# Sliding-window copy: the large DMA packets of all three rings doubled in size, and the direct ring's mix of copies made uniform

## The chip, the cores and the metric

The kernel runs on one core of a Trainium2 chip. The metric is the device time of the core in microseconds. Runs of one kernel mostly agree within 0.3%, and all runs used here are of the fast state or, where a kernel ran once, of unknown state (said there).

## The reference

Every batch of 4096 rows of 256 floats is cut into 127 overlapping windows of 64 rows, 32 rows apart. Nothing is computed; it is all copying.

```python
def setup_inputs():
    batch, length, dim = (32, 4096, 256)
    window_size = 64
    stride = 32
    return {'x': np.random.randn(batch, length, dim).astype(np.float32), 'window_size': window_size, 'stride': stride}

def reference(x, window_size, stride):
    batch, length, dim = x.shape
    n_windows = (length - window_size) // stride + 1
    result = np.zeros((batch, n_windows, window_size, dim), dtype=np.float32)
    for i in range(n_windows):
        start = i * stride
        result[:, i] = x[:, start:start + window_size].copy()
    return result
```

A block of 32 rows is 32 KB and lies twice in the output (but for the ends). A window is 64 KB, contiguous in the input and in the output. The output has 266 MB.

## The kernel before

All work is done by DMA. Three queues ("rings") feed the same 16 DMA engines, each engine having its own share of each ring:

- The **direct ring** (issued by SP) copies windows of 20 batches from HBM to HBM. A byte of output is one byte moved, one read of HBM and one write.
- The **staged ring** (issued by ACT) takes 12 batches through SBUF: one load of 4 MB and two stores of 4 MB each (blocks as first and as second halves of windows). Six tiles are loaded, then stored, then six more. A byte of output is 1.5 bytes moved, but only half a read and one write of HBM.
- The **late ring** (issued by GpSimd, a software ring) copies the windows of direct batches that staged stores overrun, 15 windows a batch, when the direct ring is nearly done.

```python
DIRECT, IN, OUT = 32768, 16384, 16384          # largest packet of each kind, bytes
...
    def windows(self, q, b, w0, n, half=None, piece=DIRECT):
        blk = self.blk
        row = [1, 2 * blk if half is None else blk]
        h = half or 0
        return q.dma_start(
            out=self.oap((b * self.nw + w0) * 2 + h, [[2 * blk, n], row]),
            in_=self.xap(b * self.nb + w0 + h, [[blk, n], row]),
            max_dma_last_dim=piece,
        )
...
    per, loads, stores = 6, 6 * 17, 34
    todo = 7 * len(direct)
    turns = share = 0
    with tc.tile_critical():
        st.run(ring_s)

        for b in direct:
            w = 0 if b - 1 not in staged else 8 if b + 1 in staged and b + 1 < B - 1 else 15
            for j in range(7):
                todo -= 1
                sem = near if todo == 2 else done
                share += 120 if turns % (loads + per * stores) < loads else 88
                if share >= 120:
                    share -= 120
                    turns += 4
                    count(c.windows(ring_d, b, w, 16, 0), done)
                    count(c.windows(ring_d, b, w, 16, 1), sem)
                else:
                    turns += 3
                    count(c.windows(ring_d, b, w, 16), sem)
                w += 16
                # ... (two small copies near the end)
        ring_r.wait_ge(near, 16)
        pieces = (32768,)
        # ... (the late ring: 15, 8 or 7 windows of each direct batch)
```

A copy of 16 windows gives each engine one window: two packets of 32 KB and one packet of 4 bytes that posts the semaphore, three turns of the ring. As two half copies it gives two packets and two semaphore packets, four turns. The code mixes the two forms, 120 of 120 halves while the staged ring loads and 88 of 120 while it stores, and so sets how many bytes the direct ring moves per turn, beside a staged ring that takes turns with it.

## Time and profile before

| | before |
|---|---|
| time, median of the first 3 runs | 753.6 us (753.49 to 754.83) |
| bytes moved by the engines | 317.56 MB |
| packets | 19,698 |
| HBM read and written | 216.86 + 267.19 MB |

From the profile's page of the kernel before: the engines' busy tenths and GB/s moved in 40 slices, then packets, MB and share of engine time by ring (q1 direct, q10 staged, q0 late), then HBM traffic:

```profile
DMA  9999999999999999999999999999999999999995
GB/s 378 429 434 434 432 423 437 422 428 430 433 439 432 426 428 437 432 423 431 424 426 433 437 433 434 427 429 429 429 433 442 425 427 431 443 426 429 420 429 223
DMA packets 19698, 317.56 MB, mean 424 GB/s; under 512 B 5214, under 2 KB 5214, under 8 KB 5422
...
q10 hardware_dynamic: 9792, 151.00, 47.2%
q1 hardware_dynamic: 8688, 147.01, 45.8%
q0 software_dynamic: 1216, 19.53, 6.1%
...
HBM read 216.86 MB, written 267.19 MB: 646 GB/s over the span
```

The engines are full until the last slice.

By stretch (window in us, its length, POOL busy, granted clock, DMA share, GB/s moved). The first two rows and the last lie in stretches in which the staged ring loads, the third in one in which it stores:

```profile
25.00:75.00 50.00, 0.00 (x0) 1.00 1.00 431
75.00:125.00 50.00, 0.00 (x0) 1.00 1.00 427
150.00:375.00 225.00, 0.00 (x0) 1.00 1.01 431
400.00:500.00 100.00, 0.00 (x0) 1.00 1.00 431
```

The rate is even, about 430 GB/s in loads and in stores alike. And the end of the run:

```profile
720.00:740.00 20.00, 0.00 (x0) 1.00 0.98 420
740.00:745.00 5.00, 0.00 (x0) 1.00 0.09 32
745.00:750.00 5.00, 0.00 (x0) 1.00 0.06 22
```

The engines stop nearly together at 740 us; one or two are some us late, and the last two windows follow.

The packet records give more:

- **The line.** Medians of a packet's duration: 4 KB 159 ns, 16 KB 611, 32 KB 1213, that is 8.5 ns plus bytes at 27.2 B/ns. A packet above its line is called slow here, and "excess" is the sum of what packets take above 611, 1213 and (later) 2418 ns, divided by 16 engines.

### The profile page before, as it was taken

To read this page: it belongs to the slowest core of one execution; us is meant where nothing else is said; L and a number is where in the kernel's file an instruction comes from. 1 tells how busy PE (TensorE), PEld (TensorE's weight loads), DVE (VectorE), ACT (ScalarE), POOL (GpSimd) and SP (SyncE) were. 2 spreads that over 40 slices of the span, in tenths; PEclk is the share of its full clock that TensorE was granted. 3 is DMA by queue.
4 is the path that set the end of the run, shared out by engine and by line. 5 is a ranking of instruction groups with operands and counts; after the bars stand their busy time and mean duration, and the time that the engine had idled before them with its cause. 6 is when DMAs were issued, how large, how long until landed. Compare 5 with 4: busy or idle time off the path is not lost.

```text
span 749.0 us, 374 instructions
## 1 busy us (share of the span) xinstructions
POOL 13.6 (2%) x27
## 2 busy tenths in 40 slices
POOL 0000000000000000000000000000000000230100
DMA  9999999999999999999999999999999999999995
GB/s 378 429 434 434 432 423 437 422 428 430 433 439 432 426 428 437 432 423 431 424 426 433 437 433 434 427 429 429 429 433 442 425 427 431 443 426 429 420 429 223
DMA packets 19698, 317.56 MB, mean 424 GB/s; under 512 B 5214, under 2 KB 5214, under 8 KB 5422
## 3 DMA queue, kind: packets, MB, share of 16 engines
q10 hardware_dynamic: 9792, 151.00, 47.2%
q1 hardware_dynamic: 8688, 147.01, 45.8%
q0 software_dynamic: 1216, 19.53, 6.1%
q14 instruction: 2, 0.02, 0.0%
HBM read 216.86 MB, written 267.19 MB: 646 GB/s over the span
## 4 chain that ended last, share of the span: by engine, by line
another core or an unknown queue 93%; POOL 2%; issue 0%; POOLq 0%; SPq 0%
POOL out_dram L34 2%; POOL out_dram L44 0%; POOLq L214 0%; SPq L141 0%; POOLq L94 0%
## 5 line engine op out<-in xcount | busy, mean ns | idle before, releaser
L34 POOL DMA_DIRECT2D out_dram<-in_x_dram x22 | 12.8, 585 | 695.3 <-DMA out_dram<-in_x_dram 649.7
L44 POOL DMA_DIRECT2D out_dram<-in_x_dram x1 | 0.6, 571 | 0.0
L200 POOL MEMSET const-float32-0.0<- 128x1 f32 x1 | 0.1, 98 | 0.2 <-issue 0.2
L200 POOL MEMSET const-bfloat16-1.0<- 128x1 bf16 x1 | 0.1, 102 | 0.0
L200 POOL MEMSET const-float32-1.0<- 128x1 f32 x1 | 0.1, 98 | 0.0
L200 POOL MEMSET const-uint8-127<- 128x1 uint8 x1 | 0.1, 98 | 0.0
## 6 DMA issues: line engine op xcount, KB each, us to landing
out_dram<-in_x_dram SPq DMA_DIRECT2D x232, 512.0 KB, 87.6
out_dram<-xb ACTq DMA_DIRECT2D x24, 4096.0 KB, 128.5
xb<-in_x_dram ACTq DMA_DIRECT2D x12, 4096.0 KB, 119.7
out_dram<-in_x_dram SPq DMA_DIRECT2D x24, 1024.0 KB, 89.6
out_dram<-in_x_dram POOLq DMA_DIRECT2D x17, 960.0 KB, 37.1
out_dram<-in_x_dram POOLq DMA_DIRECT2D x2, 512.0 KB, 43.1
out_dram<-in_x_dram POOLq DMA_DIRECT2D x2, 448.0 KB, 46.0
out_dram<-in_x_dram POOLq DMA_DIRECT2D x1, 576.0 KB, 35.4
```

The source lines that it names most:

```text
L34: return q.dma_start(out=self.oap((b * self.nw + w0) * 2 + h, [[2 * blk, n], row]), in_=self.xap(b * self.nb + w0 + h, [[blk, n], row]), m ...
L44: return q.dma_start(out=self.oap((b * self.nw + w0) * 2, [[part, 16], [2 * self.blk, n], row]), in_=self.xap(b * self.nb + w0, [[part, 16 ...
L200: nc = _bacc.Bacc("TRN2", target_bir_lowering=False, num_devices=1)
```

## The change

Twice the packet size everywhere: 64 KB direct, 32 KB staged, 64 KB late. The intent is fewer packets and half the turns on both rings, so that the balance of the rings stays. As 16 windows are then two turns (one packet, one semaphore), the two forms of copy are replaced by copies of 16 windows with, every eleventh or so, one of 32; the mix no longer depends on whether the staged ring loads or stores.

```diff
--- before.py
+++ after.py
@@ -6,7 +6,7 @@
 from concourse._compat import with_exitstack
 
 
-DIRECT, IN, OUT = 32768, 16384, 16384
+DIRECT, IN, OUT = 65536, 32768, 32768
 
 
 class Copier:
@@ -135,34 +135,31 @@
         dma.then_inc(sem, 16)
         total[sem] += 16
 
-    per, loads, stores = 6, 6 * 17, 34
     todo = 7 * len(direct)
-    turns = share = 0
+    share, singles = 0, False
     with tc.tile_critical():
         st.run(ring_s)
 
         for b in direct:
             w = 0 if b - 1 not in staged else 8 if b + 1 in staged and b + 1 < B - 1 else 15
-            for j in range(7):
-                todo -= 1
-                sem = near if todo == 2 else done
-                share += 120 if turns % (loads + per * stores) < loads else 88
-                if share >= 120:
+            wend = w + 112
+            while w < wend:
+                share += 11
+                n = 16
+                if share >= 120 and w + 32 <= wend:
                     share -= 120
-                    turns += 4
-                    count(c.windows(ring_d, b, w, 16, 0), done)
-                    count(c.windows(ring_d, b, w, 16, 1), sem)
-                else:
-                    turns += 3
-                    count(c.windows(ring_d, b, w, 16), sem)
-                w += 16
-                if todo == 7:
+                    n = 32
+                todo -= n // 16
+                count(c.windows(ring_d, b, w, n), near if todo in (2, 2 - n // 16 + 1) and total[near] == 0 else done)
+                w += n
+                if todo <= 7 and not singles:
+                    singles = True
                     count(c.windows(ring_d, B - 1, c.nw - 1, 1, 1, 2048), done)
                     if 0 in staged:
                         count(c.windows(ring_d, 0, 0, 1, 0, 2048), done)
 
         ring_r.wait_ge(near, 16)
-        pieces = (32768,)
+        pieces = (65536,)
         last = B - 2
         for i, b in enumerate(direct[:-1]):
             for g, n in enumerate(staged):
```

## The prediction

> **What bounds it now.** The 16 DMA engines, all the time. The table by 25 us windows shows a DMA share of 0.98 to 1.02 from 25 us to 725 us; in the DMA records, packet times add to about 743 us per engine, and data moves for 743.6 us. POOL is busy 2%. The bytes are fixed: 317.56 MB.
>
> What a packet costs (DMA records, medians): 2 KB 84 ns, 4 KB 159, 16 KB 611, 32 KB 1213: 8.5 ns plus bytes at 27.2 B/ns. A semaphore packet takes 9 ns. 27.2 B/ns times 16 is the 435 GB/s of the Trainium skill, "DMA: Bandwidth & Descriptors", section "Where 436 GB/s comes from"; this trace agrees. At that rate the bytes alone need 730 us. The rest of the profiled 749: data packets' fixed cost (14,482 x 8.5 / 16 = 7.7 us), semaphore packets (2.9 us), 5.5 us before the first packet, slow packets, and a tail: engines finish between 749.6 and 754.1, then two last windows follow.
>
> **What changes.**
> - Removed: half the large packets: direct ring 4480 to 2240, staged ring 9216 to 4608, late (software) ring 578 to 289. 7137 x 8.5 ns / 16 = 3.8 us.
> - Removed: the direct ring's DMAs fall from 259 to 132 (118 of 16 windows, 11 of 32, 3 small), so some 2030 semaphore packets go: 1.1 us.
> - Nothing added, if the line holds at 64 KB (2418 ns), twice the largest packet in the trace.
> - Moved: the balance of rings. The same page, section "Queues, rings and completion order", says that an engine round-robins between rings by packet. The trace agrees if semaphore packets count as turns: in a store stretch the direct ring got 176 data packets per 25 us, about 328 turns, the staged ring 304, about 323. By turns the direct ring moved 1.11 times the staged ring's bytes before (measured about 1.09); after, 33.6 KB a turn against 29.1: 1.15, corrected by that miss about 1.14. So the direct ring ends about 20 us sooner (now 664 us of the span), with the staged ring about 21 MB short of its end (before about 16). The late ring has 16.7 MB that wait only for tile stores up to the tenth; while it moves about 14 MB the eleventh is stored, so it shouldn't starve. The staged ring is alone for perhaps the last 7 us; at the start it ran alone for 3.7 us at nearly full rate.
>
> **On the critical path.** All of the saved engine time, as nothing else limits; the tail of some 6 us stays, since engines carry the same bytes and rows. 3.8 + 1.1 = 4.9 us, 0.65%: 753.6 to about 748.7 us, range 745.5 to 751.5. Faster by over 2%: 2%; within 2%: 93%; slower by over 2%: 5%.
>
> **What would show each step.**
> - Packets in all: about 10,550 (19,698 before); 64 KB packets at about 2418 ns, 32 KB staged ones at 1213.
> - GB/s in the 40 slices: up by 2 to 3 in the middle.
> - The direct ring's last packet near 645 us of the span; the late ring starting before it.
> - DMA share about 1.0 to about 740 us, then a tail of 5 to 7 us.
>
> **What would make it wrong.**
> - 64 KB packets over the line: 1% on direct packets costs 4 us.
> - One ring alone not filling the engines: each lost 10% of the last 7 to 15 us costs about 1 us.
> - The late ring's rows falling on the engines more unevenly: a packet is now 2.4 us, so the tail may grow by that much.
> - The late ring starving before the eleventh tile is stored.
> - A gain over 8 us would mean that larger packets save more than their fixed cost.

## More of the kernel before

Reads and writes of HBM are more than the bytes moved, since a direct byte counts twice.

- **Engines.** The records don't name the engine, but the next packet of an engine starts 3 to 4 ns before the last one ends, so packets can be chained; that yields 16 chains with few swaps. In before each chain has 35 to 38 half-window packets of the late ring.
- **Direct part.** The part of the bytes moved that the direct ring moved: 0.512 and 0.515 in the two load stretches, 0.535 and 0.528 in the stores. HBM traffic is the bytes moved times one plus this part: 652 GB/s in loads, 661 in stores.

## The result, and the profile after

| | before | after |
|---|---|---|
| time, median of 6 runs each | 753.97 us (753.49 to 754.83) | 766.75 us (764.91 to 770.51) |
| ratio, 95% interval | 1 | 1.0172 (1.0148 to 1.0196) |
| packets | 19,698 | 10,465 |
| excess, us per engine | 2.4, and 4.7 in a second profile (e0) | 13.5 |

The kernel is 1.7% slower; 748.7 was predicted, with 751.5 as the upper end. The same page of after:

```profile
DMA  9999999999999999999999999999999999999982
GB/s 370 413 429 422 422 425 411 430 432 430 429 426 435 418 425 423 439 432 422 430 389 417 429 429 432 420 417 427 437 427 434 411 437 434 430 435 427 408 386 123
DMA packets 10465, 317.54 MB, mean 415 GB/s; under 512 B 3119, under 2 KB 3119, under 8 KB 3327
...
q10 hardware_dynamic: 5184, 151.00, 46.7%
q1 hardware_dynamic: 4416, 147.01, 45.3%
q0 software_dynamic: 864, 19.53, 6.0%
...
HBM read 216.86 MB, written 267.19 MB: 633 GB/s over the span
```

The packets have gone as predicted (about 10,550 were expected), and the engines are again "full" until the end. But the GB/s row is lower and ragged, where 2 to 3 GB/s more had been predicted for its middle, and the last two slices are poor. A busy share of 1.00 only says that an engine always has a packet in hand; it doesn't say that the packet moves at the line. HBM traffic fell from 646 to 633 GB/s.

The same stretches as before, and the end:

```profile
25.00:75.00 50.00, 0.00 (x0) 1.00 1.00 419
75.00:125.00 50.00, 0.00 (x0) 1.00 1.01 426
150.00:375.00 225.00, 0.00 (x0) 1.00 1.00 429
400.00:500.00 100.00, 0.00 (x0) 1.00 1.00 423
```

```profile
720.00:740.00 20.00, 2.11 (x4) 1.00 0.94 405
740.00:745.00 5.00, 0.00 (x0) 1.00 0.78 333
745.00:750.00 5.00, 0.00 (x0) 1.00 0.53 225
750.00:755.00 5.00, 0.00 (x0) 1.00 0.43 184
755.00:760.00 5.00, 0.00 (x0) 1.00 0.17 70
760.00:765.00 5.00, 0.00 (x0) 1.00 0.09 26
```

In the first stretch 419 GB/s instead of 431, in the last load stretch 423 instead of 431, in stores 429 instead of 431. And the engines do not stop together any more: from 745 to 750 us only half of them are busy, the last one ends at 759, and the last two windows follow.

The packet records split the difference. The profile of before shown above is a lucky one: its span is 749.0 us, while the core's time of the timed run of that kernel is 751.7. A second profile (e0, below) spans 752.2 us and serves for the sums. Times are of the records' own clock, 10.5 us ahead of the span's: before's first packet is at 12.5 there and at 2.0 in the span. (The prediction took the two to be some 7 us apart; hence its 5.5 us before the first packet and its direct ring ending at 664 us, where the span has 2.0 and 661.) The mean end is the mean over the 16 engines, with their idle gaps near the end taken off; the tail is what the last engine ends after it. The last two windows come after the tail and aren't in it.

| us | before (e0) | after | difference |
|---|---|---|---|
| last byte | 759.3 | 771.7 | +12.4 |
| mean end of the engines | 752.9 | 759.1 | +6.2 |
| tail | 4.4 | 10.7 | +6.3 |
| excess of slow packets | 4.7 | 13.5 | +8.8 |

So there are two losses, and they are of about the same size: packets above the line (8.8 us, of which the saved packets give back some 2.7), and a tail.

**The tail.** In the chains of after, the late ring's 289 rows of 64 KB lie like this: four engines carry 22 rows, three 21, one 19, seven 17, and one none. That is just what comes out if every copy of n rows starts at the same engine: seventeen copies of 15 rows, two of 8, two of 7, one of 4. In before the same rows, as pairs of 32 KB, are even.

**Slow packets.** In after the direct part is 0.538 in the first load stretch and 0.542 in the first stores, 0.540 and 0.538 in the second ones. Mean durations are 2459 ns for the 64 KB direct packets (line 2418) and 1240 for the 32 KB staged ones (line 1213); the medians are on the line. Slow packets take 3.3 and 2.7% of the time in load stretches, 1.6 and 1.0% in stores; in before 0.2 to 0.3% in loads.

Three reasons stood to be told apart for the slow packets: the larger direct part (more HBM traffic), the length of the packets, and the loss of an even step. In before the engines keep step: in the first load stretch 14 or more of the 16 are in direct packets at once for a quarter of the time, and at most two for another quarter. The number of engines in direct packets has a standard deviation of 6.1 there; in after it falls from 4.5 to about 2.

### The profile page after: what moved, and what is told of

Same layout as the page of the kernel before. It is cut to its first block, busy times and chain, and to the rows that moved or that the text cites. A ratio compares the mean times of both kernels' runs of the same rounds, so it can differ in the third digit from the quotient of the medians.

```text
span 764.5 us, 247 instructions
## 1 busy us (share of the span) xinstructions
POOL 12.2 (2%) x27
## 2 busy tenths in 40 slices
DMA packets 10465, 317.54 MB, mean 415 GB/s; under 512 B 3119, under 2 KB 3119, under 8 KB 3327
## 4 chain that ended last, share of the span: by engine, by line
another core or an unknown queue 94%; POOL 2%; issue 0%; POOLq 0%; SPq 0%
POOL out_dram L34 1%; POOL out_dram L44 0%; POOLq L211 0%; SPq L140 0%; POOLq L94 0%
```

## The experiments

Sixteen kernels ran. Except where said, each gave the right result and was timed in 3 rounds beside before. Stretches of loads and stores, direct parts and excess are taken from the packet records as above, from one trace of each kernel; "up to 620 us" leaves out the late ring's part of the run. Code cuts are shown against after, unless said; "..." and words in <> stand for what is left out.

### e1_late32: the late ring back at 32 KB

```diff
-        pieces = (65536,)
+        pieces = (32768,)
```

> The kernel after, with only the late (software) ring's rows put back to 32 KB pieces. Theory A: with 64 KB rows the late ring's rows fall on the same engines each time (in the records of after, as far as chains of back-to-back packets show, four engines carried 22 rows, one none), with 32 KB pieces they rotate (36 to 38 half rows on each in before). Then the rows are even again, the engines end within some 6 us of each other instead of 51, and the time falls by 7 to 9 us, from 766.8 to about 759. The slow packets stay (direct mean about 2459 ns against 2418, staged about 1240 against 1213). Rival B: the tail comes from engines driven apart by the slow packets, and the rows don't matter: less than 2 us gained. The recorded prediction's even rows would make no difference either.

Measured: 764.9 us, ratio 1.0153 (1.0137 to 1.0170). The late rows are even (33 to 38 half rows in each chain) and the tail is 4.4 us instead of 10.7, as theory A has it. But the time fell by 2 us only. A late copy now takes 3 turns of an engine for 64 KB, where the staged ring takes 2 and a rare semaphore turn, so the late ring gets only 0.39 of the bytes from 665 to 750 us of the records' clock (0.54 over that part in before). The staged ring ends at 756, and the late ring is alone until 770. Late packets took 1319 ns on average instead of 1213. The edit took one loss away and brought another. The size of the gain in time is a miss of theory A.

### e2_before_late64: before, with the late ring at 64 KB

The cut is against before; it is the whole edit.

```diff
-        pieces = (32768,)
+        pieces = (65536,)
```

> The kernel before, with only the late ring at 64 KB pieces. Theory A: the same uneven rows (22 on four engines, none on one) in a kernel without slow packets: 6 to 9 us slower than before, about 761, packets on the other rings still at 1213 and 611 ns. Rival B: within 2 us of before.

Measured: 763.64 us, ratio 1.0134 (1.0119 to 1.0149). One line of the change alone costs 10 us of its 13. Excess is 5.6 us (e0: 4.7), and the mean end of the engines is 754.0 us (e0: 752.9), so it isn't slow packets, nor the late ring's fewer turns; the tail is 12.8 us (e0: 4.4). The end of the run:

```profile
720.00:740.00 20.00, 2.25 (x4) 1.00 0.93 395
740.00:745.00 5.00, 0.00 (x0) 1.00 0.53 224
745.00:750.00 5.00, 0.00 (x0) 1.00 0.44 188
750.00:755.00 5.00, 0.00 (x0) 1.00 0.15 64
755.00:760.00 5.00, 0.00 (x0) 1.00 0.10 33
```

It looks like the end of after. The loss is a little above the expected 6 to 9 us. Theory A holds: with 64 KB rows the late ring loads some engines more than others, and the tail grows by that.

### e3_direct32_staged32 and e4_direct64_staged16: one packet size at a time

```diff
-DIRECT, IN, OUT = 65536, 32768, 32768
+DIRECT, IN, OUT = 32768, 32768, 32768
...
+            for n in (64, 16, 16, 16) if b == direct[-1] else (112,):
+                count(c.windows(ring_d, b, w, n), near if n == 64 else done)
...
-        pieces = (65536,)
+        pieces = (32768,)
```

> Direct ring at 32 KB packets (one DMA of 112 windows per batch, so that the rings stay about balanced: 30.6 KB a turn against 29.1), staged ring at 32 KB, late ring at 32 KB. If each ring's own packet size makes its packets slow: staged excess stays near 27 ns a packet (7 us per engine), direct excess near 2 ns, about 754 to 757 us. If the 64 KB direct packets disturb both: all at the line, about 749 to 750. If it is any loss of the even step between engines: excess on both, about 8 to 11 us per engine in all, about 758.

Measured: 759.85 us, ratio 1.0085. The direct part was 0.51. Up to 620 us the excess is 4.5 us per engine (before: 1.8 and 3.6 in its two profiles; after: 13.2), shared by both rings: mostly at the line, but not quite. After that the staged ring ends at 726 and the late ring is alone until 765 at 1433 ns a packet, another 8 us of excess. None of the three expectations fits as it was written: they spoke of packet sizes alone and had no place for the end.

```diff
-DIRECT, IN, OUT = 65536, 32768, 32768
+DIRECT, IN, OUT = 65536, 16384, 16384
...
+                fill += 88
+                if fill >= 100:
+                    fill -= 100
+                    count(ring_d.dma_start(out=<16 x 4 bytes, side by side, of a scratch tensor>, in_=<16 x 4 bytes of x>), done)
...
-        pieces = (65536,)
+        pieces = (32768,)
```

> Direct ring at 64 KB packets, staged ring at 16 KB; tiny 4-byte-per-engine copies to a scratch tensor fill turns of the direct ring so that the rings stay balanced (about 17.4 KB a turn against 15.4). Late ring at 32 KB. If each ring's own size matters: direct excess near 40 ns a packet (5.5 us per engine), staged near 1 ns, about 757. If the 64 KB direct packets disturb both: excess on both, staged packets too. If the staged 32 KB packets were the cause: all at the line, about 752.

Measured: 950.88 us, ratio 1.263. Useless for its question: 123 fillers, whose 4-byte packets have a median of 9 ns in the records, went with direct packets of 3133 ns on average and staged ones of 773. The filler is a hazard in itself (see the last section).

### e5_late32_early: e1, with an earlier start of the late ring

```diff
-                count(c.windows(ring_d, b, w, n), near if todo in (2, 2 - n // 16 + 1) and total[near] == 0 else done)
+                count(c.windows(ring_d, b, w, n), near if todo <= 10 and total[near] == 0 else done)
...
-        pieces = (65536,)
+        pieces = (32768,)
...
-        count(c.windows(ring_r, last, 112, 4), rest)
+        count(c.windows(ring_r, last, 112, 4, None, 32768), rest)
```

> The kernel after, late ring at 32 KB pieces in all its row copies, and started some 40 us earlier (its semaphore is posted with 10 or fewer steps of 16 windows to go instead of 2), because in e1_late32 the late ring moved less per turn and was alone at the end (staged ring done at 754, late ring at 770 in the records). If the fixed rows of the 64 KB late ring cost 7 to 9 us and e1 only lost that gain to the late ring's smaller turns: 757 to 760. If the late ring's rows were not what the tail came from: 764 or more again. The slow packets stay in both.

Measured: 766.51 us, ratio 1.0171. The rings now end together (768 and 770) and the tail is 4.5 us, but nothing is gained: the excess is 19.5 us per engine, of which 10.9 on the staged ring. From 623 to 679 us two rings of direct copies run beside one staged ring: the direct part is 0.59, and the engines move 410 GB/s, 653 GB/s of HBM traffic. By its own words the expectation would make the late rows innocent; e2 shows that they are not. What e1 and e5 have in common is that the engines are busy to the end with packets above the line whenever direct traffic outweighs. That pointed away from packets and to HBM.

### e6_direct64_staged16_fill512: e4 with harmless fillers

The cut is against e4.

```diff
-                    count(ring_d.dma_start(out=<16 x 4 bytes, side by side>, ...), done)
+                    count(ring_d.dma_start(out=<16 x 512 bytes, 512 bytes apart>, ...), done)
```

> As e4_direct64_staged16, but each filler copies 512 bytes per engine to a place of its own, instead of 4 bytes beside one another: the 4-byte fillers cost some 200 us and hid the question. If the 64 KB direct packets are what makes packets slow: direct and staged excess together 6 to 11 us per engine, about 760 to 766 (fillers themselves about 3.5 us). If the staged 32 KB packets were the cause: excess as before (about 2.4 us), about 756. If any small write among the packets stalls the engines: still far slower, over 800.

Measured: 760.93 us, ratio 1.0086 (1.0066 to 1.0105). Fillers took 28 ns on average. Excess up to 620 us: 6.7 us per engine, staged 16 KB packets included (4.9 of the 7.6 over the whole run). So 32 KB staged packets are not needed for the slowness. But the direct part was 0.528 in loads here, above before's 0.512, so it doesn't convict the 64 KB packets either.

### e9_direct_from_sbuf: the direct ring without its HBM reads

```diff
-                count(c.windows(ring_d, b, w, n), near if ...)
+                count(<16 windows of out <- 16 rows of 64 KB of a fixed tile, partitions 0, 8, ..., 120>, near if ...)
```

> Wrong result on purpose: the direct ring's 64 KB packets are read from a fixed SBUF tile instead of HBM; all packet sizes and rings as in after (four staging tiles instead of six for room). HBM traffic of the direct ring is halved, its packets and turns are not. Theory A (HBM is near its limit, and long packets make longer bursts of double HBM traffic): direct packets fall to the line, 2418 ns, excess below 10 ns a packet, staged packets below 10 ns. Rival C (64 KB packets, or the uneven step of the engines, are slow in themselves): excess stays near 40 ns direct and 27 ns staged.

Measured: one run, 1257.12 us (state unknown; the result is wrong on purpose). Direct packets took 3930 ns on average, much more than with HBM as their source (2459 in after). Reading SBUF like this, from 16 partitions, is itself slow, so the run says nothing on HBM. Inconclusive.

### e10_direct_only: what HBM takes

```diff
-        st.run(ring_s)
-        ...                                     (mixed copies, late ring)
+        for b in range(B):
+            for w in range(0, 112, 16):
+                count(c.windows(ring_d, b, w, 16, None, 32768 if b < B // 2 else 65536), done)
+            if b == B // 2 - 1:
+                ring_d.wait_ge(done, total[done])
```

> Wrong result on purpose (windows 112 to 126 are not written): no staging; one ring copies direct, first 16 batches with 32 KB packets, then after a full wait 16 batches with 64 KB packets. Measures what HBM takes when all engines read and write it. If HBM has a limit near 670 GB/s of reads and writes together, as the end of e3_direct32_staged32 had it (335 GB/s moved by direct copies alone): both halves near 320 to 340 GB/s moved, packets about 1.3 times the line. If 64 KB packets use HBM worse: the second half clearly slower, by 2% or more. If direct copies alone run at the line (435 GB/s), HBM is no limit and theory A falls.

Measured, in one run (721.03 us, state unknown, wrong on purpose): the first row is the half with 32 KB packets, the second that with 64 KB packets.

```profile
20.00:340.00 320.00, 0.00 (x0) 1.00 1.00 329
380.00:700.00 320.00, 0.00 (x0) 1.00 1.00 331
```

Engines are busy all the time at 329 and 331 GB/s moved, three quarters of the 430 that they reach in before: **in direct copies alone, reads and writes of HBM together stop at 660 GB/s**, whatever the packet size (packets took 1586 and 3162 ns on average, 1.31 times the line). It isn't reads or writes by themselves that stop at 330: before reads 431 GB/s of HBM in loads and writes 431 in stores. The kernel before ran at 652 GB/s in loads and 661 in stores, so it stood near this figure, too, and not only at the limit of its engines. Theory A about HBM passes its test, and "64 KB packets use HBM worse" falls, at least for direct copies alone.

The 660 GB/s are a mean over many packets and no cap at every moment. In before's first load stretch, while 14 or more engines are in direct packets, they ask HBM for some 760 GB/s (an estimate: 14 x 27.2 B/ns x 2), and such packets still take 1213 to 1215 ns on average. This also speaks against the rival that an engine's own direct copies, and not HBM, are what is slow in e10.

### e11_before_mix_of_after and e12_after_mix_of_before: size and mix exchanged

e11 keeps the packets of before and takes the direct part of after (the cut is against before):

```diff
-                share += 120 if turns % (loads + per * stores) < loads else 88
+                share += 72 if turns % (loads + per * stores) < loads else 76
```

> The kernel before, packets of 32 and 16 KB as they were; only the share of windows that go in two half copies is lowered (72 and 76 of 120 instead of 120 and 88), so that the direct ring gets the part of the bytes that it had in after (0.538 in load stretches, 0.542 in store stretches, instead of 0.512 and 0.535). Theory M (HBM takes about 660 GB/s of reads and writes, as e10_direct_only measured, a bit less with loads; before already runs at 652 to 661; what slowed the packets is the mix, not their size): the load stretches fall from 431 to about 420 to 424 GB/s moved, slow packets cost 1.5 to 3% of the time there and 1% in stores, time 757 to 763. Theory S (long packets are slow, the mix is harmless): packets stay at the line, excess below 0.5% of the time, 752 to 755.

Measured: 755.91 us, ratio 1.0021 (0.9999 to 1.0044). Direct part 0.545 and 0.541 in loads, 0.538 in stores. The stretches as above:

```profile
25.00:75.00 50.00, 0.00 (x0) 1.00 1.01 426
75.00:125.00 50.00, 0.00 (x0) 1.00 1.00 420
150.00:375.00 225.00, 0.00 (x0) 1.00 1.01 430
400.00:500.00 100.00, 0.00 (x0) 1.00 1.00 425
```

In loads 2.3 and 2.1% of the time went to slow packets with packets of 32 and 16 KB: theory M holds for the packets, 5.5 us per engine more than in the first profile of before up to 620 us, 3.7 more than in e0. That is not a matter of the even step: the first half of the first load stretch was in step (standard deviation 6.0) and lost 2.0%. Over the two whole load stretches the HBM traffic is 642 and 651 GB/s, the same as in before (642 and 651): the higher direct part got no more out of HBM there. In the two store stretches it is 662 and 664 GB/s, and slow packets take only 0.4 and 0.1%. So there is no single figure of HBM traffic at which packets turn slow; in loads it is lower than what stores carry. In the time only 2 us of it show, less than theory M expected (757 to 763): the engines' mean end is 3.6 us later than in e0, and the tail, with even late rows, is 3.1 us instead of 4.4.

e12 keeps the packets of after and takes the mix of before:

```diff
-                share += 11
-                n = 16
-                if share >= 120 and w + 32 <= wend:
+                loading = turns % (loads + per * stores) < loads      # 6 * 9 turns of loads, 6 * 18 of stores
+                halves += 9 if loading else 0
+                pairs += 0 if loading else 3
+                if halves >= 100:
+                    # ... two half copies of 16 windows
+                else:
+                    n = 32 if pairs >= 100 and w + 32 <= wend and todo > 6 else 16
```

> The kernel after, packets of 64 and 32 KB; only the mix is put back to that of before: in the turns in which the staged ring loads, 9% of the direct ring's 16-window copies go as two half copies, and copies of 32 windows are rare, so the direct ring's part should be about 0.512 in loads and 0.53 in stores. The late ring stays as in after, with its uneven rows. Theory M: the load stretches return to 428 to 432 GB/s with under 0.7% lost to slow packets, the stores likewise; of the 11 us per engine at least 7 come back, time 756 to 760 (the uneven rows remain). Theory S: slow packets as in after, 764 to 767.

Measured: 761.10 us, ratio 1.0089 (1.0067 to 1.0110), against 1.0172 for after. Direct part 0.507 and 0.510 in loads, 0.533 in stores.

```profile
25.00:75.00 50.00, 0.00 (x0) 1.00 1.00 426
75.00:125.00 50.00, 0.00 (x0) 1.00 1.00 423
150.00:375.00 225.00, 0.00 (x0) 1.00 1.00 430
400.00:500.00 100.00, 0.00 (x0) 1.00 1.00 428
```

Half of the loss in time is gone by restoring the mix alone, with 64 KB packets everywhere and the uneven late rows (tail 10.4 us). But theory M expected under 0.7% of slow packets in loads, and 2.9 and 1.6% are left, and HBM traffic over the whole load stretches is only 626 and 644 GB/s. So length counts as well. Excess up to 620 us, in us per engine:

| | mix of before | mix of after |
|---|---|---|
| packets of before (32 and 16 KB) | 1.8 and 3.6 (two profiles) | 7.3 (e11) |
| packets of after (64 and 32 KB) | 8.3 (e12) | 13.2 |

The two effects are of like size and nearly add up, within the 2 us by which two profiles of one kernel differ.

### e13_after_mix_late32: e12 with the late ring at 32 KB

The cut is against e12.

```diff
-        pieces = (65536,)
+        pieces = (32768,)
...
-        count(c.windows(ring_r, last, 112, 4), rest)
+        count(c.windows(ring_r, last, 112, 4, None, 32768), rest)
```

> e12 and the late ring at 32 KB pieces. Rows are even then, but a late row copy takes 3 turns for 64 KB beside the staged ring's 29 KB a turn, so the late ring gets only about 0.43 of the bytes and is alone at the end, where HBM lets direct copies move 330 GB/s instead of 430. Theory M: a gain over e12 of 2 to 5 us at most, 753 to 757. If the late ring's share doesn't matter: the full 8 us, 748 to 750.

Measured: 762.11 us, ratio 1.0102 (1.0076 to 1.0128): no gain over e12. The tail fell from 10.4 to 4.8 us, but the staged ring ended at 738 and the late ring was alone until 767, with packets at 1392 ns. That the late ring would be alone at the end was foreseen; that this would take the whole gain was not (753 to 757 us was expected).

### e7_before_out_of_step and e14_after_low_mix_in_loads: step or length?

e7 breaks the even step of before: its first 16 windows go in copies of 2, 4, 8 and 16 rows of uneven length, so that the low engines start late. The cut is against before.

```diff
+                if todo == 7 * len(direct) - 1:
+                    at = 0
+                    for k, size in ((2, 320), (4, 1280), (8, 3584), (16, 11200)):
+                        for first in range(0, 16, k):
+                            count(<k rows of `size` floats, from float `at` of each window>, done)
+                        at += size
```

> The kernel before, but its first 16 direct windows go in copies of uneven length on 2, 4, 8 and 16 engines, so that the low engines are pushed 1 to 2 us out of step with the others from the start (before: nearly all 16 are in direct packets at once, or none). Packet sizes and mix as before. Rival L (the long packets only break the even step, and it is the broken step that makes packets slow): load stretches lose 2% or more to slow packets from the start, 3 us per engine or more over the run above the 2.4 of before. Theory B (length of the packets itself, in a mix near HBM's limit): the load stretches stay below 0.7%, excess over the run below 4 us per engine; the time rises only by the 2 to 4 us by which the low engines are late.

Measured: 756.70 us, ratio 1.0028 (0.9999 to 1.0056). Slow packets took 0.4% of the first load stretch (at a direct part of 0.478) and 1.1% of the second (0.520); excess up to 620 us 4.8 us per engine, and 8.9 over the whole run, 3.4 of it in the late ring, which was alone for the last 10 us. This lies between the two expectations. The better witness is e0: that run of before fell out of step by itself (standard deviation from 6.7 down to 1.8 to 2.1 after 502 us) and lost 0.03 and 0.36% in the two halves of the last store stretch, less than e12's 0.5 and 0.6% there at the same mix (0.53) and about the same deviation. So the broken step may add a little, but it doesn't carry the 8 us of e12.

e14 holds the direct ring far down in the load stretches, by fillers of 512 bytes, and keeps the packets long (the cut is against e12):

```diff
-                halves += 9 if loading else 0
+                fill += 32 if loading else 0
...
-                if halves >= 100:
-                    # ... two half copies
+                if fill >= 100:
+                    # ... one filler of 16 x 512 bytes to scratch
```

> e12 with the direct ring held far lower in the load stretches, by fillers of 512 bytes per engine (27 ns each) instead of half copies: direct part of the bytes about 0.44 to 0.46 there, so HBM is asked for some 625 GB/s at the line. Packets stay at 64 and 32 KB. Theory B' (long packets lower the HBM demand at which packets turn slow): the loss to slow packets in the load stretches falls from 2.9 and 1.6% (e12) to below 0.7%. If long packets beside loads are slow whatever HBM is asked for: 1.5% or more stays. The time itself rises, as the direct ring is left with more at the end; it isn't the question.

Measured, one run (773.56 us, state unknown): direct part 0.433 and 0.441, HBM at 610 and 620 GB/s. Slow packets take 1.7% in the first load stretch (2.5% in its first half, when the engines are still in step, 0.9% in its second) and 0.5% in the second load stretch. Against e12's 2.9 and 1.6% that is less in both, and in the second it meets the expectation; in the first it doesn't. So long packets beside loads turn slow at a lower HBM demand than short ones, most of all while all engines take their long direct packets at once. By which mechanism stays open, and single traces are a weak witness here: in its store stretches, with no fillers and the mix of e12, e14 lost 1.4% where e12 lost 0.8 and 0.6%.

### e0_before_again, e15_after_rows_in_turn, e16_mix_and_rows

> The kernel before, unchanged, to see how much its profile varies: the trace first shown spans 749.0 us, 2.7 less than the core's time in the timed run, which no later trace does. All theories: time within 0.3% of before; trace span 750 to 753, slow packets 2 to 5 us per engine, part of bytes of the direct ring 0.51 in loads and 0.53 in stores.

Measured: 753.86 us, ratio 0.9996; trace span 752.2 us, excess 4.7 us, direct part 0.513 and 0.514 in loads. The unchanged kernel varies by some 2 us of slow packets from run to run, and the first profile was a good one.

e15 is after with its late rows in pairs, 64 KB packets as they were:

```diff
-                count(c.windows(ring_r, b, w, n, None, pieces[i % len(pieces)]), rest)
+                count(<rows w+i and w+i+n//2: [[2*blk, n//2], [2*blk*(n//2), 2], [1, 2*blk]]>, rest)
+                if n % 2:
+                    count(c.columns(ring_r, b, w + n - 1, 1), rest)
```

> The kernel after, 64 KB packets on the late ring too; but its rows go in pairs (rows i and i + n/2 on one engine, a three-dimensional copy), the odd row in 4 KB columns on all 16 engines. Theory A (a two-dimensional copy of n whole rows starts at the same engine each time, a three-dimensional one starts where the last one ended): each engine carries 8 or 9 pairs, 16 to 18 rows, no engine is left without, the tail (last engine over the mean of the engines) falls from 10.7 to 4 to 7 us, slow packets stay, time 760 to 764. If the engines are fixed for pairs too: seven engines carry nearly all late rows, the tail grows past 30 us and the time past 785.

Measured: 766.81 us, ratio 1.0175. The rows go round (14 to 19 in each chain, none left out) and the tail falls to 5.1 us, as expected. The time does not fall. The end of the run:

```profile
720.00:740.00 20.00, 0.00 (x0) 1.00 1.03 358
740.00:745.00 5.00, 0.00 (x0) 1.00 1.09 351
745.00:750.00 5.00, 0.00 (x0) 1.00 0.91 286
750.00:755.00 5.00, 0.00 (x0) 1.00 0.61 211
755.00:760.00 5.00, 0.00 (x0) 1.00 0.19 79
```

The late copies, in pairs and columns with more turns, got only 0.30 of the bytes while the staged ring ran. That ring ended at 742 in the records' clock, 732 in the span's. From 740 to 745 us the engines are all busy with little but the late ring. The view has 351 GB/s there at a DMA share of 1.09, as it counts a packet where it starts; spread over the packets' durations it is 318, near e10's 330. Late packets took 2793 ns on average instead of 2418, 6.3 us of excess. What the even rows gave, the mix at the end took.

> e12 (mix of before restored) and the rows of e15 together: both repaired parts at 64 and 32 KB packets. Parts add: e12 is at 761.1, the tail gives back 4 to 6 us: 755 to 758. What is left over before (753.8) is then the slow packets of the longer packets themselves, some 4 us less their saved fixed cost. If 64 KB packets had no cost of their own: 751 to 753, below before.

e16 is the edit of e12 and that of e15 together. Measured: 765.41 us, ratio 1.0154 (1.0127 to 1.0181), where 755 to 758 was expected: a miss by 8 us. The parts do not add, for the reason just seen: the staged ring ended at 729, the late ring worked alone for 41 us, and its packets took 2874 ns. The late ring of e16 needs more turns than that of e12, and with a slower direct ring ahead of it still more direct work was left for an end that runs at e10's rate (329 GB/s from 720 to 745 us of the span).

No kernel of these beats before.

## Why the prediction was wrong

1. *"All of the saved engine time, as nothing else limits"*: this is the step that failed. In place of 4.9 us saved, packets above the line cost 8.8 us per engine more than in e0, and HBM is what limited besides the engines: direct copies alone stop at 660 GB/s of reads and writes together (e10), and in loads HBM gave e11 no more than before, some 650, though it was asked for more. Before's own page shows 646 GB/s over the span, and its store stretches ran at 661. The line was on the page and was not weighed. The Trainium skill, "HBM Reference", section "Specifications (TRN2)", gives about 716 GB/s for the HBM that two cores share; no load or store stretch of any run here got beyond about 665 GB/s.

2. *"Moved: the balance of rings"* was counted in turns and seen only as a matter of which ring ends when. Its size was off too: 1.14 times the staged ring's bytes was expected, 0.538 to 0.542 of all bytes is 1.16 to 1.18 times. What mattered was not asked: each direct byte asks HBM for two, each staged byte for one. At the engines' line, some 433 GB/s, the direct part of after asks HBM for 433 x 1.538 = 666 GB/s in loads; it got 646. e11 shows the mix alone costing 3.7 to 5.5 us of slow packets per engine (against the two profiles of before), e12 shows half of the loss in time undone by restoring it. The expression that the diff removed, 120 in loads and 88 in stores, kept the direct part low in loads, where e11 has its slow packets. The rings didn't end as foreseen either: the direct ring's last packet was expected 20 us earlier than in before, near 645 us of the span, and came 5.5 us earlier, at 656 (661 in before).

3. *"Nothing added, if the line holds at 64 KB (2418 ns)"*: the line held for the median, exactly, and not for the mean. With the mix of before, longer packets still cost 4.7 to 6.5 us per engine (e12 against e0 and before, up to 620 us). That HBM takes 64 KB packets as well as 32 KB ones when there is nothing else (e10) rules out a general inefficiency; e14 shows less loss in loads when HBM is asked for less there, in one trace. Longer bursts on a memory at its limit is the reading that fits, but only argued.

4. *"the tail of some 6 us stays, since engines carry the same bytes and rows"*: wrong, and by one line of the diff. Whole rows of 64 KB make the late ring's copies two-dimensional, and in the chains of after those all start at one engine (0 to 22 rows); rows cut in two, or taken in pairs, go round (e1: 33 to 38 half rows, e15: 14 to 19 rows). e2 shows 10 us for that line alone. The Trainium skill, "DMA: Bandwidth & Descriptors", section "Why a DMA increments its semaphore by 16 and not by 1", has both cases: software-ring copies go to "k consecutive engines (mod 16) from a round-robin cursor", except that some direct copies get k = 16 with the rows (the page says partitions) dealt out from engine 0 on. The chains agree: 0 to 22 rows in after, 35 to 38 half rows in before (which engine by number a chain is, they don't show). The prediction had uneven rows among its risks, but at 2.4 us; the tail grew by 6.3 us in after and by 8.4 in e2.

5. The saving itself was mis-sized. 8.5 ns is a packet's recorded duration beyond its bytes; but the next packet starts 3 to 4 ns before the last has ended, so a packet costs about 4.5 ns and a semaphore packet about 5.5. 7137 x 4.5 ns and 2030 x 5.5 ns over 16 engines are 2.7 us, not 4.9. The sum then closes for the engines' mean end: 8.8 us of excess less 2.7 is 6.1; 6.2 was measured (e0 against after).

What was right: the number of packets, the removed semaphores, the medians, and that only the engines' work could change the time.

Open: why long packets beside loads turn slow at a lower HBM demand; why packets turn slow in loads at a lower HBM traffic than stores carry; how much the loss of the even step adds to it; and a version with even 64 KB late rows that also keeps its share of turns, which was not found.

## What to carry to other kernels

Where copies from HBM to HBM run beside copies through SBUF, compute HBM traffic (bytes moved times one plus the direct part) beside bytes moved, and ask of a change to packet sizes or turns what it does to the mix in every stretch, the end included. A DMA share of 1.00 hides slow packets: compare durations, mean against median, not occupancy. And when the shape of a DMA changes, look up and check on which engines its rows land.

## What the Trainium skill lacked or had wrong

- "HBM Reference", section "Specifications (TRN2)": it says that one core streaming alone is bounded by its 16 engines at about 425 GB/s. Copies from HBM to HBM on one core alone stopped short of that: 330 GB/s moved, 660 GB/s of reads and writes (e10), at both packet sizes. The page has no figure for such copies.
- "DMA: Bandwidth & Descriptors", section "Why a DMA increments its semaphore by 16 and not by 1": it says that "some direct copies" on the software ring get fixed engines, not which. Here two-dimensional copies of 15, 8, 7 and 4 rows of 64 KB did (0 to 22 rows per engine), three-dimensional ones of the same rows as two 32 KB pieces or as pairs of rows went round (35 to 38 half rows; 14 to 19 rows).
- The same page, section "Specifications", asks for 512 B at least for line rate and gives no time for what is below. 123 copies of 16 x 4 bytes, side by side in HBM, made the kernel 190 us slower than 123 copies of 16 x 512 bytes, 512 bytes apart (e4 950.9, e6 760.9): about 1.5 us each. Size and neighbourhood were changed together, so which of them it is stays open.
- "DMA: Bandwidth & Descriptors" has no figure for how far packets overlap in a trace: on one engine a packet starts 3 to 4 ns before the last one's recorded end, so durations make the fixed cost of a packet look nearly twice what it is (8.5 against 4.5 ns, an estimate from these records).
